# A decoder layer on one core: S5's outputs paused at the ninth batch, GLA heads cut in three, and the gate's adaLN loads spread anew

## The chip, the cores and the metric

The kernel runs on one core of a Trainium2 chip. The metric is the device time of one execution in microseconds (us). The core has a matrix engine (TensorE, PE in the profile; its weight loads are shown as PEld), a vector engine (VectorE, DVE), a scalar engine (ScalarE, ACT), a general engine (GpSimd, POOL) and a sync engine (SP) that here only issues DMAs. Each engine runs its own instructions strictly in the order in which they were written into its program, and waits at the first one whose inputs are not there. Sixteen DMA engines move data between the chip's memory and the on-chip buffer.

## The reference, cut to what matters

One layer of a hybrid decoder, in float32, with 256 tokens and a width of 4096:

```python
mod = silu(c) @ w_ada + b_ada;  shift, scale, gate = split(mod)      # adaLN, c is one row
h = x * (1 + scale) + shift
q, k, v, g_lr, z_gla, u_s5, z_s5 = split(h @ w_in)
# GLA, 4 heads: causal gated linear attention, RMS norm per head, times silu(z_gla)
# S5, 128 groups of 16 channels: s_t = A s_{t-1} + B u_t (complex, diagonal, 64 states)
y = gelu(Re(C s) + D u_s5);  y = y * sigmoid(y @ w_glu + b_glu);  o_s5 = y * silu(z_s5)
mixed = concat(o_gla, o_s5) @ w_out
out = layer_norm(ALPHA * x + gate * mixed)
```

Nearly all the weight traffic is w_ada (4096 x 12288), w_in (4096 x 10256), w_out (4096 x 4096) and w_glu (2048 x 2048). Only the product with w_ada has a single row on the left.

## The kernel before, in words

**Loads.** All large weights come in loads of 512 KB (128 partitions x 1024 numbers; two narrow chunks use less), issued on SP's queue into six buffers that all of them share in turn (raw, L81). A load of w_in, w_out or w_glu is split into two parts for a more exact product: ACT rounds it to hi (L114), DVE forms the rest as lo (L115). PE then multiplies three times, hi by hi, hi by lo and lo by hi. For w_in and w_out this is 12 matmuls of 512 columns a load (L211, L738), for w_glu 24 of 256 columns (L591). A load of w_ada goes to DVE alone: one instruction (L153; L151 for the first of a piece) multiplies it by its values of silu(c) and adds it to a running sum, rows, of which there is one buffer. 32 loads are a piece of 1024 columns; at its end PE sums over partitions with matmuls by a column of ones (L166 for shift and scale, L720 for gate). Pieces 0 to 7 are shift and scale, pieces 8 to 11 the gate, which is wanted only near the end.

**Stages.** First comes piece 0. Then w_in is multiplied in eight blocks b of the contraction, block by block as the pieces 1 to 7 arrive. It has 21 chunks of columns (KINDS, L45): four of u, S5's input; four of zs, S5's gate; then, for each of the four GLA heads, qk, v and zg (head 0's v is in two parts, va and vb). In the last block, b = 7, all chunks become final, the first eight (u and zs) with two loads each, the next six chunks with two, the last seven with four. A finished u chunk is turned by PE (L246) and rearranged by ACT with 32 small copies (L416); a finished zs chunk is turned and put through silu. Then follow: w_out's first half, on GLA's outputs (64 loads, eight chunks cc of eight); the GLU (32 loads); w_out's second half, on S5's outputs (64 loads); and the layer norm.

**S5** is a generator that is advanced beside the loads. s5_inputs makes the inputs of the state sums in 16 batches, and drives the first scan, of half of the states (scans[0]). s5_outputs then goes through the 16 batches again: s5_states (L506) multiplies the states by C on PE, s5_lags has PE turn a small matrix (L519) and ACT copy it out in 16 pieces (L522), and a last product (L552), an addition on DVE (L553) and 16 gelu pieces on ACT (L559) give y. A scan (s5_scan, L472) is a chain of 63 steps of four small DVE instructions (L479 to L482), each step on the one before. Batches 0 to 7 need scans[0]; batches 8 to 15 need scans[1], which s5_outputs itself drives, 12 steps an iteration, from its first iteration (L540, L547).

**Order.** Nothing of this order is fixed by the source alone. Each instruction has a priority, its place in the source, moved back by later(n); a planner, which runs ahead of time with its own idea of durations, puts together each engine's program from the instructions that it takes to be ready, by priority. The main function (hymba_layer) sets how fast the side work is brought in. Stages.step adds a rate to a sum and advances its generator by the whole steps in it. S5 gets RATES = (1.3, 0.85): s5_inputs 1.3 steps for each step of w_in's last 13 chunks (38 steps in all), s5_outputs 0.85 for each load of w_out's first half. The gate's w_ada loads (gate_steps, 128 loads and each piece's end) get GATE_RATES: 1.2 in the last block's u and zs chunks, 0 in the GLA chunks, 1.3 in w_out's first half from its fourth chunk on (nine steps a chunk), 0.9 for each GLU load, 0.7 in w_out's second half.

**GLA.** gla_head(h), L608, is one plain function, called after head h's zg chunk. It makes the decays (an exp, a log, an exp on ACT, L623 to L637; two scans on DVE, L628), turns q and k (L246), forms the attention matrix (L657, L661, L663), multiplies it by v (L670), norms and gates (L672 to L676), turns the result (L684) and splits it into hi and lo (L687, L688), which w_out's first half multiplies by.

Of the kernel before, what the change touches and what calls it, by code (L numbers as in the profile page):

```python
# [35 lines left out]

ADA_LEAD = 1

RATES = (1.3, 0.85)
GATE_RATES = (1.2, 0, 1.3, 0.9, 0.7)  # L40

PAIRED = (6, 7, 7, 7, 7, 8, 7)


KINDS = (  # L45
    [("u", i) for i in range(4)]
    + [("zs", i) for i in range(4)]
    + [("qk", 0), ("va", 0), ("vb", 0), ("zg", 0)]
    + [c for h in range(1, 4) for c in (("qk", h), ("v", h), ("zg", h))]
)  # L50
# [7 lines left out]
class Emit:  # L58
# [465 lines left out]
    def s5_outputs(self):  # L524


        nc = self.nc
        nb = NPAIR // NB
        self.y = []
        self.ct_next = None  # L530
        self.dd = [self.cp.tile([P, NB, 32], F32, name=f"dd{i}") for i in range(2)]
        for t in self.dd:
            nc.gpsimd.memset(t, 0.0)
        self.s5_prep(0)
        yield
        nxt = None
        for b in range(-1, nb):
            ys = nxt
            with self.later(-BG_LATE):
                drive(self.scans[1], 6)  # L540
            if b + 1 < nb:
                kt, nxt = self.s5_states(b + 1)
            if b + 2 < nb:
                self.s5_prep(b + 2)
            yield
            with self.later(-BG_LATE):
                drive(self.scans[1], 6)  # L547
            if b >= 0:
                o = self.zbank([P, NB, 64])
                for n in range(NB):  # L550
                    pr = b * NB + n
                    nc.tensor.matmul(o[:, n], lhsT=self.w0[b % 2][:, n], rhs=self.u4[pr // 16][:, pr % 16, :], start=True, stop=True)  # L552
                nc.vector.tensor_tensor(out=o, in0=o, in1=ys, op=ALU.add)  # L553
                if b % 4 == 0:
                    self.y.append(self.slot([P, 4, SEQ], name="y"))
                yv = self.y[-1][:, b % 4].rearrange("p (j c) -> p j c", j=4)
                for a in range(NB):
                    for j in range(4):
                        nc.scalar.activation(out=yv[32 * a : 32 * a + 32, j], in_=o[32 * j : 32 * j + 32, a], func=AF.Gelu_apprx_tanh)  # L559
                yield  # L560
            if b + 1 < nb:
                self.s5_lags(b + 1, kt)
                yield
# [42 lines left out]


    def gla_head(self, h):  # L608
        nc = self.nc
        v = nc.vector  # L610
        qk = self.acc["qk"][h]
# [49 lines left out]
        v.tensor_copy(out=att[:, 1], in_=ap[:, 1])  # L661
        for i in (0, 2):
            v.copy_predicated(att[:, i], self.causal.bitcast(U32), ap[:, i])  # L663
        zg = self.acc["zg"][h]
        ss = self.tmp([P, 2], "ss")
        ops = []
# [8 lines left out]
        for it in range(2):  # L675
            v.scalar_tensor_tensor(out=zg[:, it], in0=ops[it], scalar=rs[:, it : it + 1], in1=zg[:, it],  # L676
                                   op0=ALU.mult, op1=ALU.mult)
        o = zg
        hi = self.slot([P, 4, SEQ], F32R, "ohi")
        lo = self.slot([P, 4, SEQ], F32R, "olo")  # L680
# [131 lines left out]
def drive(g, n=1):  # L812

    for _ in range(n):
        if next(g, "end") == "end":
            return False
    return True
# [24 lines left out]
def chain(*gs):  # L842
    for g in gs:
        yield from g


def win_plan():

    nch = len(KINDS)
    paired = [[]]  # L850
    for b in range(1, 8):
        n = PAIRED[b - 1]
        paired.append(list(range(nch - n, nch) if b % 2 == 1 else range(n)))
    paired.append([])
    plan = []
    for b in range(8):
        pairs = [(n, [b - 1, b]) for n in paired[b]]
        alone = [(n, [b]) for n in range(nch) if n not in paired[b] + paired[b + 1]]
        plan.append(alone + pairs if b == 7 else pairs + alone)
    return plan  # L860


@with_exitstack
def hymba_layer(ctx: ExitStack, tc: tile.TileContext, io):
    em = Emit(tc, ctx, io)
    em.h = {}
    em.part = {}
    em.consts()
    em.alloc_acc()
    em.stats = em.cp.tile([P, 2, 8, 6], F32, name="stats")  # L870
    em.oh, em.ol = [None] * 8, [None] * 8

    drive(em.ada_steps(0), 99)
    with em.later(LATE):
        em.s5_params()
        em.ln_rows()
    em.u4 = []
    s5 = Stages((em.s5_inputs(), RATES[0]), (em.s5_outputs(), RATES[1]))
    nch = len(KINDS)
    ada = chain(*[em.ada_steps(u) for u in range(1, 8)])  # L880
    plan = win_plan()
    marks, at = [], 0
    for b, visits in enumerate(plan):
        marks.append(at)
        at += sum(len(us) for _, us in visits)
    marks[0], pos, done = 0, 0, 0
    gt = Stages((em.gate_steps(), 1))
    for b, visits in enumerate(plan):
        for n, us in visits:
            last = us[-1] == 7  # L890
            em.win_chunk(n, us, us[0] == 0, last)
            pos += len(us)
            want = round(33 * np.interp(pos + ADA_LEAD, marks, range(8)))
            drive(ada, want - done)
            done = max(done, want)
            kind, i = KINDS[n]
            steps = range(len(us) if kind in WIDTHS else 2 * len(us))
            if b == 7:
                for _ in steps:
                    gt.step(GATE_RATES[0] if n < S5_AT else GATE_RATES[1])  # L900
            if last and n >= S5_AT:
                with em.later(LATE):
                    for _ in steps:
                        s5.step()
                if kind == "zg":
                    em.gla_head(i)
    for cc in range(8):
        for i, _ in enumerate(em.wout(cc, 0)):
            if i < 8:
                with em.later(BG_LATE):  # L910
                    s5.step()

                gt.step(GATE_RATES[2] if cc > 2 else 0)
    s5.finish()
    em.glu_prepare()
    for cc in range(8):
        for _ in em.glu_chunk(cc):
            gt.step(GATE_RATES[3])
    left = []
    for cc in range(8):  # L920
        for i, _ in enumerate(em.wout(cc, 1)):
            gt.step(GATE_RATES[4])
            if i == 4 and left and len(em.gates) > left[0] // 2:
                em.residual(left.pop(0))()
        left.append(cc)
    gt.finish()
    for cc in left[:-1]:
        em.residual(cc)()
    em.layer_norm(em.residual(left[-1]))
# [69 lines left out]
```

## Time and profile before

| | us |
|---|---|
| median of three runs | 1723.9 (1722.66 to 1725.07) |
| the profiled execution, its own time | 1730.86 |
| its span, first to last instruction | 1729.1 |
| PE busy, of the span | 1546.0 (89%) |
| DVE busy | 1461.6 (85%) |
| ACT busy | 829.7 (48%) |
| mean share of the DMA engines | 78% (queues 1 and 0 together) |
| mean granted TensorE clock | 0.963 of full |

The profile is of one execution. A group of instructions is shown with its line, engine, operation, what it writes and reads, its count, its busy time and the mean of one, and then the idle time of its engine just before it with the engine that ended most of it. Matmuls are pipelined and overlap in the profile, so a PE that is shown busy need not be at its peak. A view by stretches gives, for each stretch, its length, the busy time and the count of instructions of PE, PEld, DVE, ACT and POOL, the clock granted to TensorE, the share of the DMA engines and the GB/s.

By the marks in the trace the last block's u and zs chunks end near 900, the GLA chunks near 1053, w_out's first half near 1415 (the GLU's first matmul is at 1415.29), the GLU near 1505, the gate's loads near 1625, and w_out's second half near 1700.

### The profile page before, as it was taken

The page shows a single profiled execution, that of the slowest core. Times are in us where ns is not written, and L with a number is a line of the kernel's source. Part 1 is how long each engine was busy: PE and PEld are TensorE (multiplying, and loading weights), DVE is VectorE, ACT ScalarE, POOL GpSimd, SP SyncE. Part 2 cuts the span into 40 slices and gives each one's busy share as a digit, 9 for nine tenths or more (in the row PEclk, how much of TensorE's full clock was granted, in tenths as well). Part 3 has the DMA queues.
Part 4 walks back from the last instruction along what each step waited for, and adds up shares of the span by engine and source line. Part 5 has one row for each costly group of instructions (what it writes and reads, how often), then busy time and mean ns, then how long its engine had stood idle before and what let it go on. Part 6 is the DMA issues. An engine that isn't in the chain of part 4 may idle for free.

```text
span 1729.1 us, 22283 instructions
## 1 busy us (share of the span) xinstructions
PE 1546.0 (89%) x7548; PEld 1285.3 (74%) x7548; DVE 1461.6 (85%) x2096; ACT 829.7 (48%) x1468; POOL 67.2 (4%) x134
## 2 busy tenths in 40 slices
PE   0689999999999999998989999889749889999995
PEld 0577878888888888877768888668637669977783
DVE  6899889898998999988867689979876779989975
ACT  0345434343343433433687767458538835433330
POOL 1000000000000000000001000000000000010100
PEclk9999999999999999999999999979969999999996
DMA  9999999999999999999876343317516899999962
GB/s 351 346 352 348 357 323 351 338 338 347 344 347 338 342 358 333 335 312 315 291 251 211 115 145 123 106 54 236 198 40 206 282 364 326 372 345 345 346 191 97
DMA packets 138067, 480.65 MB, mean 278 GB/s; under 512 B 17899, under 2 KB 18363, under 8 KB 137691
## 3 DMA queue, kind: packets, MB, share of 16 engines
q1 hardware_dynamic: 130240, 457.85, 74.0%
q0 software_dynamic: 7712, 21.37, 3.8%
q8 instruction: 59, 0.97, 0.2%
q14 instruction: 56, 0.46, 0.1%
HBM read 472.77 MB, written 6.39 MB: 277 GB/s over the span
## 4 chain that ended last, share of the span: by engine, by line
PE 65%; DVE 12%; ACT 9%; DMA 7%; issue 6%; SPq 0%; DVEq 0%; ACTq 0%
PE mm L211 42%; PE mm L738 13%; DVE rows L153 5%; DVE lo L115 3%; DMA raw<-in_ada 3%; ACT hi L114 2%; ACT u L416 2%; ACT w L522 2%; PE mm L591 2%; DMA raw<-in_w_out 2%; ACT y L559 2%; PE pz L506 2%; DMA raw<-in_w_glu 2%; PE pz L465 1%; PE px L166 1%
## 5 line engine op out<-in xcount | busy, mean ns | idle before, releaser
L114 ACT CAST hi<-raw 128x1024 fp32r<-128x1024 f32 (+2 forms) x496 | 506.6, 1025 | 626.2 <-DMA raw<-in_w_in 212.3
L115 DVE TENSOR_TENSOR lo<-raw,hi 128x1024 fp32r<-128x1024 f32 (+2 forms) x496 | 583.6, 1186 | 103.7 <-ACT hi L114 95.3
L211 PE MATMUL mm<-hi,hhi 128*128 128x512 f32 (+2 forms) x1344 | 512.8, 385 | 24.3 <-ACT hi L114 17.6
L211 PE MATMUL mm<-hi,hlo 128*128 128x512 f32 (+2 forms) x1344 | 511.5, 383 | 0.0
L153 DVE SCALAR_TENSOR_TENSOR rows<-raw,silu_c,rows 128x1024 f32<-128x1024 f32 x372 | 476.2, 1280 | 28.7 <-DMA raw<-in_ada 25.3
L211 PE MATMUL mm<-lo,hhi 128*128 128x512 f32 (+2 forms) x1344 | 353.1, 385 | 1.8 <-DVE lo L115 1.7
L211 PEld LDWEIGHTS mm<-hi,hhi 128*128 128x128 f32 x1344 | 254.8, 190 | 74.9 <-ACT hi L114 19.8
L211 PEld LDWEIGHTS mm<-hi,hlo 128*128 128x128 f32 x1344 | 255.0, 190 | 47.5
L211 PEld LDWEIGHTS mm<-lo,hhi 128*128 128x128 f32 x1344 | 247.2, 190 | 51.3 <-DVE lo L115 4.5
L738 PE MATMUL mm<-hi,ohi 128*128 128x512 f32 x512 | 209.3, 410 | 18.4 <-ACT hi L114 17.1
L738 PE MATMUL mm<-hi,olo 128*128 128x512 f32 x512 | 205.9, 403 | 0.0
L738 PE MATMUL mm<-lo,ohi 128*128 128x512 f32 x512 | 142.4, 400 | 6.4 <-DVE lo L115 6.4
L738 PEld LDWEIGHTS mm<-hi,ohi 128*128 128x128 f32 x512 | 99.5, 195 | 45.8 <-ACT hi L114 23.8
L738 PEld LDWEIGHTS mm<-lo,ohi 128*128 128x128 f32 x512 | 96.3, 191 | 32.4 <-DVE lo L115 10.9
L738 PEld LDWEIGHTS mm<-hi,olo 128*128 128x128 f32 x512 | 99.8, 195 | 20.5 <-issue 0.3
L506 PE MATMUL pz<-e,pad 128*128 128x97 f32 (+1 forms) x256 | 49.6, 361 | 32.1 <-issue 26.8
L506 PEld LDWEIGHTS pz<-e,pad 128*128 128x128 f32 x256 | 46.3, 239 | 35.8 <-issue 27.2
L591 PE MATMUL mm<-yhl,hi 128*128 128x256 f32 x512 | 68.3, 287 | 3.7 <-ACT hi L114 3.7
L591 PEld LDWEIGHTS mm<-yhl,hi 128*128 128x128 f32 x512 | 64.8, 195 | 5.5 <-ACT hi L114 4.6
L166 PE MATMUL px<-ones,rows 128*128 128x1 f32 x128 | 16.5, 258 | 54.8 <-DVE rows L153 54.8
L522 ACT COPY w<-px 32x128 f32<-32x128 f32 (+3 forms) x256 | 55.5, 217 | 15.9 <-PE px L519 11.6
L166 PEld LDWEIGHTS px<-ones,rows 128*128 128x128 f32 x128 | 17.2, 209 | 55.5 <-DVE rows L153 54.8
(238 smaller groups left out, 1197.9 us busy)
## 6 DMA issues: line engine op xcount, KB each, us to landing
raw<-in_ada SPq DMA_DIRECT2D x384, 512.0 KB, 5.5
raw<-in_w_in SPq DMA_DIRECT2D x304, 512.0 KB, 5.3
raw<-in_w_out SPq DMA_DIRECT2D x128, 512.0 KB, 4.8
raw<-in_w_glu SPq DMA_DIRECT2D x32, 512.0 KB, 5.7
raw<-in_w_vb SPq DMA_DIRECT2D x16, 272.0 KB, 3.8
x<-in_xT POOLq DMA_DIRECT2D x16, 256.0 KB, 4.9
raw<-in_w_va SPq DMA_DIRECT2D x16, 256.0 KB, 4.2
xo<-in_x_tok POOLq DMA_DIRECT2D x8, 512.0 KB, 7.0
```

The source lines that it names most:

```text
L114: nc.scalar.copy(out=hi, in_=src)
L115: nc.vector.tensor_tensor(out=lo, in0=src, in1=hi.bitcast(F32), op=ALU.subtract)
L153: nc.vector.scalar_tensor_tensor(out=rows, in0=t, scalar=c, in1=rows, op0=ALU.mult, op1=ALU.add)
L166: nc.tensor.matmul(ps[:, s, kt : kt + 1], lhsT=self.rows[:, 512 * s + kt * P : 512 * s + kt * P + P], rhs=self.ones[:, 0:1], start=True, s ...
L211: nc.tensor.matmul(ps[:, m, 0:w], lhsT=t[:, 2 * half + kt, m * P : m * P + P], rhs=r[:, kt], start=st, stop=en)
L416: nc.scalar.copy(out=self.u4[i][32 * j : 32 * j + 32, 8 * half + a : 8 * half + 8 : 4, :], in_=uv[32 * a : 32 * a + 32, :, j, :])
L465: nc.tensor.matmul(eps[:, ri, :, n], lhsT=w1s[n // 2][:, n % 2, ri], rhs=self.u4[pr // 16][:, pr % 16, :], start=True, stop=True)
L506: nc.tensor.matmul(yps[:, n, 0 : moved.shape[1]], lhsT=pad[:, n, ri].rearrange("p k g h -> p (k g h)"), rhs=moved[:, :, ri, (b * NB + n) % ...
L522: nc.scalar.copy(out=w0[32 * j : 32 * j + 32, n, 32 * j : P], in_=kps[32 * n : 32 * n + 32, 0 : P - 32 * j])
L559: nc.scalar.activation(out=yv[32 * a : 32 * a + 32, j], in_=o[32 * j : 32 * j + 32, a], func=AF.Gelu_apprx_tanh)
L591: nc.tensor.matmul(ps[:, m], lhsT=w[:, kt, m * P : m * P + P], rhs=t[:, kt, :], start=u == 0 and j == 0, stop=u == 3 and j == len(todo) - 1)
L738: nc.tensor.matmul(ps[:, it], lhsT=t[:, 2 * n2 + m, it * P : it * P + P], rhs=w[:, m], start=first and j in (0, 2), stop=last and j >= len ...
```

## The change

Four things, and no instruction's size or count of the arithmetic changes:

- **S5's outputs.** The rate rises from 0.85 to 0.92 steps a load, and at the head of the iteration that makes the states of batch 8, the ninth, the generator yields nine times and does nothing.
- **GLA heads.** gla_head becomes a generator with two yields. Its first part, up to the attention matrix, is now run after the head's qk chunk (head 0: after vb); its second part, the product with v, the norm and the gate, after the zg chunk, where the whole head stood; its third, the turn and the split, one chunk later, and for the last head after four loads of w_out's first chunk.
- **u and zs.** Their eight chunks come in turn: u0, zs0, u1, zs1 and so on. Their loads' order in memory follows.
- **The gate's loads.** The rates become 1.2, 0.4, 1, 0.9 and 0.6.

```diff
-RATES = (1.3, 0.85)
-GATE_RATES = (1.2, 0, 1.3, 0.9, 0.7)
+RATES, PAUSE = (1.3, 0.92), 9
+GATE_RATES = (1.2, 0.4, 1, 0.9, 0.6)
...
-    [("u", i) for i in range(4)]
-    + [("zs", i) for i in range(4)]
+    [c for i in range(4) for c in (("u", i), ("zs", i))]
...
         for b in range(-1, nb):
             ys = nxt
+            if b == 7:
+
+                for _ in range(PAUSE):
+                    yield
             with self.later(-BG_LATE):
                 drive(self.scans[1], 6)
...
             v.copy_predicated(att[:, i], self.causal.bitcast(U32), ap[:, i])
+        yield
         zg = self.acc["zg"][h]
...
                                    op0=ALU.mult, op1=ALU.mult)
+        yield
         o = zg
...
+    turn = []
...
+                if turn:
+                    drive(turn.pop(), 9)
+                if kind == "vb" or kind == "qk" and i:
+                    head = em.gla_head(i if kind == "qk" else 0)
+                    drive(head)
                 if kind == "zg":
-                    em.gla_head(i)
+                    drive(head)
+                    turn.append(head)
...
                 gt.step(GATE_RATES[2] if cc > 2 else 0)
+                if cc == 0 and i == 3:
+                    drive(turn.pop(), 9)
```

## The prediction, made before the changed kernel was run

> **What bounds the kernel now.** I read the page first, for the engines and their slices, then stretches of it by stage, then the instructions around the largest gap.
>
> ```profile
> PE 1546.0 (89%) x7548; PEld 1285.3 (74%) x7548; DVE 1461.6 (85%) x2096; ACT 829.7 (48%) x1468; POOL 67.2 (4%) x134
> PE   0689999999999999998989999889749889999995
> PEclk9999999999999999999999999979969999999996
> DMA  9999999999999999999876343317516899999962
> ```
>
> PE is the busiest engine, but slices 20 to 32 hold its gaps, and there DMA is nearly empty. The stretches, with length first, then PE, PEld, DVE, ACT, POOL, clock, DMA share and GB/s:
>
> ```profile
> 850.00:900.00 50.00, 42.92 (x200) 34.44 (x199) 35.56 (x30) 45.88 (x143) 1.63 (x3) 0.93 0.77 249
> 900.00:1053.00 153.00, 153.00 (x866) 129.14 (x865) 113.76 (x234) 108.55 (x163) 12.43 (x26) 1.00 0.50 161
> 1053.00:1141.00 88.00, 76.01 (x388) 61.27 (x386) 80.73 (x290) 46.22 (x73) 4.92 (x11) 0.94 0.34 107
> 1141.00:1243.00 102.00, 94.80 (x457) 81.73 (x457) 81.80 (x195) 79.33 (x273) 4.81 (x9) 0.92 0.57 187
> 1243.00:1273.00 30.00, 3.19 (x13) 2.36 (x14) 27.50 (x148) 0.00 (x0) 0.00 (x0) 0.59 0.06 18
> 1273.00:1415.00 142.00, 119.73 (x516) 94.24 (x516) 104.16 (x119) 95.59 (x314) 7.46 (x13) 0.89 0.70 242
> 1505.00:1625.00 120.00, 113.70 (x521) 91.58 (x520) 108.80 (x100) 44.81 (x45) 10.07 (x19) 1.00 0.96 350
> 1625.00:1700.00 75.00, 74.53 (x324) 59.85 (x322) 50.39 (x48) 25.32 (x25) 4.79 (x9) 1.00 0.57 185
> ```
>
> The w_out first half is the weak stage. The four rows from 1053 to 1415 add to 362 us with PE busy for 293.7 and DVE for 294.2: both are idle for 68 us, in turn. The largest gap:
>
> ```profile
> 1272.82 0.50 PE L506 MATMUL pz<-e,pad 128*128 128x96 f32 x1 [26.81 <-issue]
> 1272.49 0.22 DVE L482 TENSOR_TENSOR e<-sc,sc 128x64 f32<-128x64 f32 x1
> L482 DVE TENSOR_TENSOR e<-sc,sc 128x64 f32<-128x64 f32 x34 | 7.6, 225 | 1.2
> ```
>
> The last row groups DVE from 1246 to 1273. The profile names "issue", but PE's next instruction is batch 8's states, and it starts 0.1 us after the scan step that ended at 1272.71. DVE did 34 steps in that gap and nothing else, 0.79 us a step. So the gap is the second scan, late; ACT, SP and the loads stood still behind it.
>
> One load of w_out costs PE 12 matmuls. In the last stretch, which is nearly all w_out, 324 took 74.53 us: 0.230 each, 2.76 a load. A w_ada load, 512 KB at the 350 GB/s of 1505 to 1625, is 1.5 us of DMA and 1.28 of DVE; the groups of DVE from 1053 to 1415, and in the last row w_ada's from 1142 to 1243:
>
> ```profile
> L115 DVE TENSOR_TENSOR lo<-raw,hi 128x1024 fp32r<-128x1024 f32 x63 | 76.8, 1220 | 32.9 <-ACT hi L114 32.0 <-PE mm L738 0.6 <-issue 0.2
> L153 DVE SCALAR_TENSOR_TENSOR rows<-raw,silu_c,rows 128x1024 f32<-128x1024 f32 x51 | 65.2, 1277 | 2.9 <-DMA raw<-in_ada 2.5
> L153 DVE SCALAR_TENSOR_TENSOR rows<-raw,silu_c,rows 128x1024 f32<-128x1024 f32 x13 | 16.6, 1275 | 1.5 <-DMA raw<-in_ada 1.3
> ```
>
> **The change part by part.** The sum is made against the profiled execution's own 1730.86 us (span 1729.1); the median of the runs is 7 below it, and I carry the difference over unchanged.
>
> *The pause.* Nine empty steps at 0.92 a load are 9.8 loads; PE has 9.8 x 2.76 = 27.0 us to do where it now stands for 26.8. What is queued behind batch 8's states on PE is w_out's matmuls, and with them ACT's hi, DVE's lo and SP's loads; these come in front of it. The price is on DVE: 9.8 loads bring 9.8 x 1.22 of lo and, at the new rate of 1, 9.8 x 1.28 of rows, 24.5 us, beside 34 steps x 0.79 = 27. Behind all of it the states would come some 25 us later, yet with ten loads more done. Bounds: 0, if the planner still lets PE wait as long, to -26.8. I take **-26.8**, since DVE's stretch of 1505 to 1625 shows 91% busy beside a PE at 95%.
>
> *The clock after it.* A stall is paid twice:
>
> ```profile
> 1270.00:1280.00 10.00, 7.18 (x27) 5.38 (x27) 6.60 (x25) 1.80 (x8) 0.05 (x1) 0.50 0.00 1
> 1280.00:1290.00 10.00, 8.43 (x44) 6.87 (x43) 6.06 (x11) 7.99 (x37) 2.53 (x5) 0.87 0.21 66
> 1290.00:1300.00 10.00, 6.37 (x19) 4.84 (x20) 9.78 (x13) 9.33 (x40) 0.48 (x1) 0.66 0.61 181
> ```
>
> Busy time by the share of the clock that was missing: 7.18 x 0.50 + 8.43 x 0.13 + 6.37 x 0.34 = 6.9 us. Some of it belongs to later small gaps; **-5**, bounds 0 and -6.9. The Trainium skill, "TensorE: Matmul & The Clock Gate", Part 1: The HAM clock gate, says that an idle array falls to half clock and is released after about 3.4 us of steady work: one restart would cost an estimated 1.7 us and the whole sum would be 3.3 us smaller. The three rows show a clock below full for longer, and I keep the rows.
>
> *GLA in parts.* The last head's chain now lies wholly before w_out's first chunks can end:
>
> ```profile
> 1089.31 1.28 ACT L624 ACT_TABLE_LOAD   x1
> 1123.40 0.48 PE L684 MATMUL px<-ident,zg 128*128 128x128 f32 x1 [4.16 <-DVE zg L676]
> 1141.76 0.58 PE L506 MATMUL pz<-e,pad 128*128 128x97 f32 x2 [3.74 <-DVE e L482]
> wg<-in_w_gla_gate POOLq DMA_DIRECT2D x4, 16.0 KB, 2.4
> ```
>
> From 1053 to 1141 PE is idle for 88 - 76.0 = 12.0 us. Of this 3.7 is the wait of batch 0's states for the first scan; the rest, 8.3, lies in and around head 3. With its first part two chunks (eight loads, 22 us) earlier, most goes: **-8**, bounds 0 and -12. Each head's small load (2.4 us to landing) and its two fills on POOL's queue move with its first part, past loads of S5's parameters; the 22 us hide them, and without that cover the head pays the 2.4. The tables that ACT loads are as many as before.
>
> *The gate's loads.* By the rates, w_out's first half has 45 instead of 58.5, the GLA chunks 38 x 0.4 = 15.2 instead of none, and the tail 19.8 after the GLU instead of 21.5, over 33 loads instead of 31. In w_out's first half DVE loses 13.5 x 1.28 = 17.3 us; PE gains only where DVE is last: **-4**, bounds 0 and -17.3. In 900 to 1053 PE is full, DMA half empty and DVE 39 us idle, so the 15.2 x 1.28 = 19.5 us fit; but each new load takes one of the six buffers on SP's queue until DVE is done with it, ahead of w_in's. **+4**, bounds 0 and +19.5. In the tail (1505 to 1625: DMA 0.96, DVE 91%) a load's share falls by 0.1 x 1.5 us, over 33 loads 5: **-3**, bounds 0 and -5.
>
> *u and zs in turn.* From 850 to 900 ACT is the bound, 45.9 of 50:
>
> ```profile
> L416 ACT COPY u<-px 32x128 f32<-32x128 f32 x127 | 32.7, 257 | 1.6
> PE px L246 <- ACT u L416: 7.1, 5, 2.4
> ```
>
> The 128 copies come in a run and PE loses 50 - 42.9 = 7.1 us to them. Spread over eight chunks they need the same 33 us, over 16 loads x 2.76 = 44 us of PE: **-4**, bounds 0 and -7.1.
>
> *S5's end.* It has 50 steps, over 0.85 that is 58.8 loads; 59 over 0.92 is 64.1, all 64. What is late next is the last y, which the GLU needs:
>
> ```profile
> 1373.16 1.05 ACT L572 CAST yhl<-y 128x1024 fp32r<-128x1024 f32 x1
> 1415.29 0.38 PE L591 MATMUL mm<-yhl,hi 128*128 128x256 f32 x1 [2.04 <-ACT hi L114]
> L522 ACT COPY w<-px 32x128 f32<-32x128 f32 (+1 forms) x117 | 25.4, 217 | 8.7 <-PE px L519 6.1
> L559 ACT ACTIVATE y<-pz 32x64 f32<-32x64 f32 x112 | 24.1, 215 | 2.8 <-DVE pz L553 1.5
> ```
>
> Now the last cast of y begins 42 us before the GLU. Batches 8 to 15 took from 1273 to 1373. A last batch with nothing beside it is 16 x 0.217 + 16 x 0.215 = 6.9 us of ACT with a few us of PE and DVE between: **+8**, bounds 0 and +15.
>
> **Sum:** -26.8 - 5 - 8 - 4 + 4 - 3 - 4 + 8 = -38.8; 1730.9 - 38.8 = 1692 for an execution like the profiled one, 1723.9 - 38.8 = **1685** for the median. A second way, by S5 alone: batch 8 comes 24.5 us later for the paused loads, 8 earlier for head 3, and 4 earlier for the 13 rows that become 10, so some 12 us after 1273; its last y is 12 us after 1373, and a GLU right behind it starts 30 us before 1415. With u and zs, the tail and the GLA chunks, -4 - 3 + 4, that is 1691, within the range below.
>
> **The rivals.**
>
> *A. DVE takes the stall's place.* It is 92% busy both in 1053 to 1141 and in the gap. If the paused loads' 24.5 us push the scan back by as much, PE waits in many small pieces for DVE's lo instead of once for the scan, at the same cold clock, and of the first half's gains only DVE's saved rows count: -17.3 + 4 - 3 - 4 + 8 = -12, **1712**. Against it: the same rows show 68 us of idle DVE in the stage. By the Trainium skill, "Perfetto Trace Analysis", Identifying the Most-Contended Engine, occupancy is a fair measure for VectorE; it would name DVE in 1053 to 1273 and so speaks for this rival.
>
> *B. Slower: S5's chain outruns its cover.* The 15 rows in the GLA chunks push the first scan back by up to 19.5 us, the pause adds 27.0, and the last y comes 46.5 us later, near 1420. From 42 us on it is S5 and no longer w_out that sets the GLU's start, and all gains before it are lost; PE has no load left beside the last two batches, each 6.9 us of bare ACT: 4.5 + 13.8 = 18, against 7 saved in u, zs and the tail: +11, **1735**. For it: 64.1 steps for 64 loads. Against it: DVE's 39 idle us before 1053.
>
> *C. The pause does not do what it says.* The planner lets PE wait for the states behind the paused loads as long as before: the 26.8 and the 5 stay, and with S5's end at its bound the rest is -8 - 4 + 4 - 3 - 4 + 15 = 0: **1724**. For it: the wait of the profile was planned too, since DVE's program holds the 34 steps in one piece.
>
> *D. More.* DVE's 294.2 us in w_out's first half fall by 17.3; at the 91% of 1505 to 1625 the stage takes 305 us, 57 less; with -4 - 3 + 4 that is **1664**.
>
> **How the numbers follow.** The forecast has 0.53 (its own range 1668 to 1702), A 0.20, B 0.12, C 0.07, D 0.08. A change of 0.2%, 3.4 us, is about what a measurement of this kernel can tell from none. Faster is the forecast, A and D, 0.81; same is C, 0.07; slower is B, 0.12. The low end, 1652, is D with the bounds of the clock, 6.9, and of u, zs and the tail, 5; the high end, 1722, is A with S5's end at its bound, 7, and 3 more for the rows in the GLA chunks. The range leaves out B and most of C.
>
> **What would show it.** PE's wait before batch 8's states is under 5 us, with some ten more of w_out's loads done by then; the clock stays above 0.9 in the stage; in 1053 to 1141 no wait of PE on head 3 is above 2 us; 900 to 1053 has about 15 rows on DVE and PE still above 97%; the time from the last cast of y to the GLU's first matmul falls from 42 us to below 20. The forecast is wrong if that wait stays above 15 us, if PE in the GLA chunks falls below 90%, or if the GLU's start waits for y.

## The result and the profile after

The changed kernel takes 1703.25 us (median of four runs, 1702.25 to 1706.66) beside 1724.49 for the kernel before on the same chip: a ratio of 0.9866, 95% interval 0.9848 to 0.9883. It is 21 us faster by the medians and 23 by the ratio; 39 were forecast. Where parts are weighed against one another below, the ratio is taken, times 1725. The profiled execution took 1702.25, its span is 1700.4, so it stands 1 us below its median, whereas the one of before stood 7 above: between the two profiles lie 28.7 us, between the medians 21.

The page of the kernel after, engines and slices:

```profile
PE 1535.8 (90%) x7548; PEld 1282.5 (75%) x7548; DVE 1455.3 (86%) x2096; ACT 827.4 (49%) x1468; POOL 66.4 (4%) x134
PE   0689999999999999999899999869995879999995
PEclk9999999999999999999999999979997789999996
DMA  9999999999999999998997643314894079999962
```

Slices 26, 27 and 31 to 33 (42.5 us each) still hold holes in PE and in the clock, and DMA reads 1 and 0 at the bottom of them. The stretches of the kernel after, with the columns of before (length, PE, PEld, DVE, ACT, POOL, clock, DMA share, GB/s):

```profile
830.00:889.00 59.00, 55.35 (x274) 45.32 (x274) 52.33 (x49) 49.80 (x138) 3.79 (x7) 1.00 0.92 319
889.00:1053.00 164.00, 159.62 (x921) 134.67 (x921) 134.35 (x274) 116.05 (x188) 12.18 (x26) 1.00 0.58 188
1053.00:1141.00 88.00, 67.72 (x310) 51.60 (x310) 79.43 (x294) 38.46 (x72) 6.13 (x14) 0.85 0.31 97
1141.00:1287.00 146.00, 144.44 (x683) 121.51 (x681) 129.06 (x270) 101.50 (x286) 4.29 (x8) 0.98 0.76 264
1287.00:1306.00 19.00, 0.74 (x4) 0.38 (x3) 16.37 (x82) 2.09 (x2) 0.00 (x0) 0.64 0.30 99
1306.00:1330.00 24.00, 18.00 (x78) 16.91 (x78) 10.69 (x23) 16.61 (x73) 1.07 (x2) 0.50 0.02 6
1330.00:1384.00 54.00, 47.24 (x223) 39.21 (x222) 28.60 (x38) 46.45 (x179) 3.06 (x6) 0.84 0.40 136
1384.00:1488.00 104.00, 98.94 (x778) 96.12 (x778) 96.39 (x87) 56.12 (x96) 4.62 (x9) 0.97 0.91 329
```

The u and zs stretch of before, for the first row:

```profile
834.00:901.00 67.00, 56.57 (x262) 45.32 (x261) 51.56 (x48) 54.45 (x155) 2.58 (x5) 0.95 0.79 265
```

And the waits that matter, from the timeline of the kernel after (L505, L481, L575 and L594 are the L506, L482, L572 and L591 of before; L744, L114 and L152, further down, are its L738, L115 and L153):

```profile
1129.48 0.74 PE L505 MATMUL pz<-e,pad 128*128 128x97 f32 x2 [14.86 <-DVE e L481]
1305.62 1.60 PE L505 MATMUL pz<-e,pad 128*128 128x96 f32 x6 [18.26 <-DVE e L481]
1383.60 0.64 PE L594 MATMUL mm<-yhl,hi 128*128 128x256 f32 x4
1397.24 1.04 ACT L575 CAST yhl<-y 128x1024 fp32r<-128x1024 f32 x1
1398.34 0.58 PE L594 MATMUL mm<-yhl,hi 128*128 128x256 f32 x1 [3.39 <-ACT yhl L575]
```

The wait before batch 8 is there as before, 18.3 us instead of 26.8, behind the same instruction of the second scan; batch 8 starts 33 us later, at 1305.6 instead of 1272.8. What has changed is how much of w_out is done by then. w_out's matmuls (12 a load) before batch 8, in the kernel before and after:

```profile
1053.00:1272.80 219.80, 121.78 (x468) 0.88 0.41 132
```

```profile
1053.00:1305.60 252.60, 166.53 (x672) 0.91 0.57 194
```

39 loads have become 56, 17 more. By stages in us, from the marks in the two traces:

| stage | before | after | difference |
|---|---|---|---|
| up to the last addition to zs | 900.5 | 888.7 | -11.8 |
| GLA chunks, to w_out's first matmul | 153.2 | 164.7 | +11.5 |
| w_out's first matmul to batch 8 | 219.1 | 252.2 | +33.1 |
| batch 8 to the GLU's first matmul | 142.5 | 78.0 | -64.5 |
| GLU | 97.1 | 104.0 | +6.9 |
| from the GLU's last matmul to the end | 216.7 | 212.8 | -3.9 |

### The profile page after: what moved, and what is told of

Read it like the earlier page. It is cut to its first block, busy times and chain, and to the rows that moved or that the text cites. A ratio compares the mean times of both kernels' runs of the same rounds, so it can differ in the third digit from the quotient of the medians.

```text
span 1700.4 us, 22243 instructions
## 1 busy us (share of the span) xinstructions
PE 1535.8 (90%) x7548; PEld 1282.5 (75%) x7548; DVE 1455.3 (86%) x2096; ACT 827.4 (49%) x1468; POOL 66.4 (4%) x134
## 4 chain that ended last, share of the span: by engine, by line
PE 61%; DVE 16%; ACT 9%; DMA 8%; issue 5%; SPq 0%; DVEq 0%; ACTq 0%; POOLq 0%
PE mm L210 40%; PE mm L744 11%; DVE rows L152 5%; DMA raw<-in_ada 4%; DVE lo L114 4%; PE mm L594 4%; ACT hi L113 2%; ACT y L562 2%; ACT w L521 2%; DMA raw<-in_w_in 2%; DMA raw<-in_w_out 2%; PE pz L505 2%; PE px L165 1%; DVE sc L478 1%; DVE e L481 1%
## 5 line engine op out<-in xcount | busy, mean ns | idle before, releaser
L114 DVE TENSOR_TENSOR lo<-raw,hi 128x1024 fp32r<-128x1024 f32 (+2 forms) x496 | 582.8, 1184 | 72.5 <-ACT hi L113 66.8
L152 DVE SCALAR_TENSOR_TENSOR rows<-raw,silu_c,rows 128x1024 f32<-128x1024 f32 x372 | 475.7, 1279 | 38.6 <-DMA raw<-in_ada 35.5
L744 PE MATMUL mm<-hi,ohi 128*128 128x512 f32 x512 | 204.1, 400 | 4.9 <-ACT hi L113 4.9
L744 PE MATMUL mm<-hi,olo 128*128 128x512 f32 x512 | 202.5, 397 | 0.3 <-DVE olo L694 0.2
L744 PE MATMUL mm<-lo,ohi 128*128 128x512 f32 x512 | 141.3, 397 | 2.1 <-DVE lo L114 2.1
L744 PEld LDWEIGHTS mm<-hi,ohi 128*128 128x128 f32 x512 | 97.3, 191 | 28.3 <-ACT hi L113 7.4
L744 PEld LDWEIGHTS mm<-lo,ohi 128*128 128x128 f32 x512 | 96.2, 190 | 25.4 <-DVE lo L114 4.6
L744 PEld LDWEIGHTS mm<-hi,olo 128*128 128x128 f32 x512 | 97.4, 191 | 21.5 <-DVE olo L694 1.4
L505 PE MATMUL pz<-e,pad 128*128 128x97 f32 (+1 forms) x256 | 51.7, 375 | 33.1 <-DVE e L481 33.1
L505 PEld LDWEIGHTS pz<-e,pad 128*128 128x128 f32 x256 | 48.8, 266 | 35.2 <-DVE e L481 34.0
L594 PE MATMUL mm<-yhl,hi 128*128 128x256 f32 x512 | 70.2, 291 | 4.6 <-ACT yhl L575 3.4
L594 PEld LDWEIGHTS mm<-yhl,hi 128*128 128x128 f32 x512 | 66.5, 199 | 6.2 <-ACT yhl L575 3.6
```

What stands on the lines that cost most here:

```text
L114: nc.vector.tensor_tensor(out=lo, in0=src, in1=hi.bitcast(F32), op=ALU.subtract)
L152: nc.vector.scalar_tensor_tensor(out=rows, in0=t, scalar=c, in1=rows, op0=ALU.mult, op1=ALU.add)
L505: nc.tensor.matmul(yps[:, n, 0 : moved.shape[1]], lhsT=pad[:, n, ri].rearrange("p k g h -> p (k g h)"), rhs=moved[:, :, ri, (b * NB + n) % ...
L594: nc.tensor.matmul(ps[:, m], lhsT=w[:, kt, m * P : m * P + P], rhs=t[:, kt, :], start=u == 0 and j == 0, stop=u == 3 and j == len(todo) - 1)
L744: nc.tensor.matmul(ps[:, it], lhsT=t[:, 2 * n2 + m, it * P : it * P + P], rhs=w[:, m], start=first and j in (0, 2), stop=last and j >= len ...
```

## The experiments

**Each part alone.** The kernel before with one of the four parts.

The pause and 0.92 (e1):

```diff
-RATES = (1.3, 0.85)
+RATES, PAUSE = (1.3, 0.92), 9
...
+            if b == 7:
+                for _ in range(PAUSE):
+                    yield
```

> The kernel before with S5's new rate (0.92) and its pause of nine loads alone. If the pause is what lets PE multiply in front of batch 8's states (the pause theory, as predicted), the wait before batch 8 falls from 26.8 us to below 10 and the time falls by 15 to 25 us. If that wait was held open by the end of a gate piece - the one buffer rows is not free, four of the six load buffers fill with w_ada, and w_out's loads stop (the piece-end theory) - the pause alone leaves it near 25 us and the time moves by less than 8 us either way.

Measured: 1733.5 beside 1727.7, ratio 1.0041 (1.0020 to 1.0061). Alone, the pause makes the kernel slower, by 7 us. Batch 8 starts at 1333, 60 us later than before, with 56 loads in front, and still after a wait of 29.7 us. The pause and the rate of 0.92 go together in every run here; "the pause" below means both, and what each does by itself was not tried.

The GLA heads in three parts (e3), the edit as in the change:

> The kernel before with GLA's heads in three parts alone. Predicted: -8 us, head 3's first part two chunks earlier. From the trace after the change, where the heads' first matmuls come at 912, 976, 1030 and 1081 us against 924, 979, 1036 and 1085 before, the other view is that the heads follow one another as before and this part brings less than 4 us.

Measured: 1725.9 beside 1727.7, ratio 0.9991 (0.9972 to 1.0011): no change that can be told from none. Inside, batch 0 starts 9 us earlier (1132.7 instead of 1141.8), but batch 8 only 2.5.

The gate's rates (e4):

```diff
-GATE_RATES = (1.2, 0, 1.3, 0.9, 0.7)
+GATE_RATES = (1.2, 0.4, 1, 0.9, 0.6)
```

> The kernel before with the gate's new rates alone. Pause theory: -4 +4 -3, so about -3 us, and batch 8 still waits 20 us or more. Piece-end theory: the piece no longer ends while batch 8 waits for the scan; PE multiplies on, more than 45 loads of w_out's first half are done when batch 8's states start (39.6 in the kernel before), and the time falls by 15 us or more.

Measured: 1727.6 beside 1727.7, ratio 0.9995 (0.9974 to 1.0017): no change that can be told from none. Yet its trace has moved: batch 8 starts at 1308.3, behind a wait of 33.2 us, with 48 loads in front instead of 39. The piece-end theory has its loads here and not its time.

u and zs in turn (e5), the new KINDS:

> The kernel before with u and zs in turn alone. Predicted: -4 us, PE's idle time of 7.1 us beside ACT's 128 copies shrinks, and the last of u and zs ends some 4 us earlier than 900.5. The other view, from the parts run so far (each alone moved the time by -2 to +7 us though their sum is -23 together): the few us are taken back where the second scan sets the start of batch 8, and the time moves by less than 3 us.

Measured: 1715.0 beside 1725.4, ratio 0.9941 (0.9918 to 0.9964). A line that the forecast priced at 4 us brings 10. Its stage ends 9 us earlier, but the GLA chunks behind it then take 167 us instead of 153, with the gate's loads as before. The groups of S5's inputs on PE in the GLA chunks, first the kernel before (901 to 1053), then u and zs alone (891 to 1058):

```profile
L465 PE MATMUL pz<-u,w 128*128 128x64 f32 x168 | 21.1, 268 | 0.0
L452 PE MATMUL pz<-ident,pad 128*128 128x128 f32 x87 | 14.6, 273 | 0.0
```

```profile
L464 PE MATMUL pz<-u,w 128*128 128x64 f32 x196 | 26.6, 275 | 0.0
L451 PE MATMUL pz<-ident,pad 128*128 128x128 f32 x100 | 15.8, 279 | 0.0
```

41 more of S5's small matmuls stand there, 6.7 of the 14 us: work has moved over the stage's edge. w_out's first matmul comes 5 us later than before, and the stage behind it is 14 us shorter (347.6 from there to the GLU, instead of 361.6). A gain that is read at one mark can be lost or doubled at the next, and only the end counts.

**Two parts together, and one part undone.** The four alone add to 7.1 - 1.6 - 0.9 - 10.2 = -5.6 us; together they give -23. So some depend on one another. The pause together with the gate's rates (e9):

> The kernel before with the pause (and 0.92 steps a load) and the gate's new spread; GLA heads and the order of u and zs stay as before. Pause alone took 1733.5 with batch 8 at 1333, gate alone 1727.6 with batch 8 at 1308. Theory: the second scan is late because rows and splits of DVE stand between its steps; with 1.0 row a load in place of 1.3 it ends earlier, batch 8 starts near 1315 with some 57 loads in front, and the pause then pays: 1712 to 1718. Rival: the gate's spread doesn't matter for the scan, which comes whenever the loads in front are through; the other two parts make the difference: batch 8 above 1328 and 1725 to 1735.

Measured: 1717.7 beside 1727.9, ratio 0.9938 (0.9923 to 0.9953). The time is the first theory's: two edits that give +7 and -1 us alone give -11 together. Batch 8 is at 1321.6, 7 us later than that theory said, again with 56 loads in front.

The changed kernel with the gate's old rates (e10):

```diff
-GATE_RATES = (1.2, 0.4, 1, 0.9, 0.6)
+GATE_RATES = (1.2, 0, 1.3, 0.9, 0.7)
```

> The changed kernel with the gate's old spread (1.2, 0, 1.3, 0.9, 0.7). Theory (rows beside the scan): batch 8 moves from 1306 to 1320 or later, and the time from 1703 to 1710 to 1716. Rival: the gate's spread is neutral, and what the rows cost in the GLA chunks (13 us) they give back in the tail: batch 8 within 5 us of 1306, 1700 to 1706. By the prediction's own terms (-4, +4, -3) 1706.

Measured: 1723.2 beside 1727.9, ratio 0.9979 (0.9967 to 0.9991). Without the gate's spread all but 4 us of the gain are gone, more than either theory gave it.

The changed kernel without the pause, at 0.85 (e2):

```diff
-RATES, PAUSE = (1.3, 0.92), 9
+RATES, PAUSE = (1.3, 0.85), 0
```

> The changed kernel with S5's old rate (0.85) and no pause; GLA's parts, u and zs in turn and the gate's new rates stay. Pause theory: it loses 15 to 25 us against the changed kernel, so it takes about 1722 us. Piece-end theory: it keeps most of the gain, 1695 to 1710 us, since the gate's new rates put the piece's end elsewhere, and S5's last batches have more loads beside them.

Measured: 1714.7 beside 1727.7, ratio 0.9927 (0.9904 to 0.9951). The pause is worth 10.5 us here, less than the pause theory gave it and more than the other, and it costs 7 where the gate is as before.

The changed kernel with each head in one go (e12), gla_head without its yields, called behind zg:

> The changed kernel with each GLA head issued in one go behind its zg, as before. The prediction gave the parts 8 us: 1711. The traces say otherwise: head 3's first matmuls came 4 us earlier than before, all of it from u and zs, and the part alone took 0.9991 of before: 1701 to 1705, with the heads' first matmuls within 3 us of 913, 976, 1030 and 1081.

Measured: 1704.0 beside 1727.9, ratio 0.9859 (0.9844 to 0.9874), the same as with the parts. Head 3's first matmul is at 1086 instead of 1081, batch 8 at 1306.3 instead of 1305.6.

Why the pause and the gate need one another is read from two stretches of each kernel: from w_out's first matmul to batch 8, and from there to the GLU. Pause alone:

```profile
1053.00:1333.00 280.00, 227.14 (x1063) 184.01 (x1062) 248.78 (x682) 146.93 (x367) 11.73 (x24) 0.89 0.58 201
1333.00:1412.00 79.00, 62.21 (x300) 53.80 (x300) 35.30 (x60) 66.05 (x263) 3.13 (x6) 0.78 0.20 62
```

Pause and gate:

```profile
1057.00:1322.00 265.00, 222.61 (x1063) 182.97 (x1062) 235.56 (x675) 149.05 (x372) 12.21 (x25) 0.91 0.55 188
1322.00:1401.00 79.00, 65.85 (x302) 56.28 (x301) 40.33 (x63) 63.96 (x255) 4.13 (x8) 0.76 0.30 97
```

The changed kernel with the gate undone:

```profile
1046.00:1317.00 271.00, 215.46 (x1023) 174.10 (x1022) 242.36 (x654) 144.90 (x364) 12.36 (x24) 0.91 0.58 206
1317.00:1396.00 79.00, 62.33 (x302) 54.14 (x303) 36.16 (x62) 66.91 (x265) 3.13 (x6) 0.78 0.20 62
```

And without the pause:

```profile
1052.00:1299.00 247.00, 193.31 (x896) 156.94 (x894) 216.36 (x634) 132.61 (x350) 10.52 (x22) 0.88 0.53 182
1299.00:1401.00 102.00, 87.28 (x406) 73.92 (x407) 52.56 (x78) 80.71 (x301) 4.66 (x9) 0.84 0.36 119
```

And the gate's rates alone:

```profile
1050.00:1308.00 258.00, 202.18 (x965) 165.62 (x963) 227.70 (x663) 140.20 (x362) 12.20 (x25) 0.89 0.51 177
1308.00:1410.00 102.00, 87.23 (x404) 74.02 (x405) 52.36 (x78) 80.57 (x301) 4.57 (x9) 0.84 0.35 116
```

The first stretch has DVE busy for 88 or 89% of it in all five; in the kernel before it is 190.0 of 220, 86% (the prediction's rows from 1053 to 1273), in the changed one 224.9 of 253, 89%. In order of length the seven kernels are in order of DVE's work, from 190 to 249 us, but not of PE's. The second stretch does not go with DVE's work: it is 142 us long with 25 loads left, 102 with 16 and 78 or 79 with 8, and DVE is idle for about half of the short ones. So each load that the pause brings forward in the kernel before saves 63 / 17 = 3.7 us behind and costs DVE's lo and its share of the rows in front. The rows instructions on DVE before batch 8, in the kernel before, with the pause alone, and with pause and gate (length, DVE busy and count, clock, DMA share, GB/s):

```profile
1053.00:1273.00 220.00, 16.57 (x13) 0.88 0.41 132
```

```profile
1053.00:1333.00 280.00, 56.22 (x44) 0.89 0.58 201
```

```profile
1057.00:1322.00 265.00, 39.61 (x31) 0.91 0.55 188
```

With 17 loads more, lo takes 17 x 1.22 = 21 us more; the rows take 40 more with the old rates and 23 with the new. That is 61 and 44 us of DVE, and the stretch grew by 60 and 45. Against 63 saved behind, and 7 or 4 lost in the GLU to a later last y, the pause alone gains nothing, and with the new rates it gains some 14 in the profile. Most of the missing rows (12) are done in the GLA chunks. The gate's rates alone already put 9 loads and 18 rows more in front than before, which makes the first stretch 38 us longer and the second 40 shorter. The pause on top of them adds 8 loads and no row: the first stretch grows by 7 us, the second shrinks by 23 and the GLU grows by 5, a gain of 11.

**The second scan taken away.** If DVE is the bound before batch 8, the second scan's 44 us there (56 steps of 0.79) should come off the time; if the pause only covers the late scan, it should be worth nothing without it. The second scan is cut to 7 of 63 steps in the changed kernel (e6), and in the one without the pause (e7):

```diff
-        for c in range(1, 64):
+        for c in range(1, 8 if h else 64):
```

> The changed kernel with the second scan cut to 7 of its 63 steps, so 56 x 0.79 = 44 us of DVE work are left out. If the second scan's end is what starts batch 8 (the scan theory), the 18.3 us wait goes, batch 8 starts 30 us or more earlier, and the time falls by 10 to 25 us. If something else holds batch 8 or the GLU, the time falls by less than 5 us.

> The changed kernel without pause and with S5's old rate, and with the second scan cut to 7 steps as in the run beside it. If the pause pays only because it puts loads in front of a late scan, it is worth nothing here: this run is within 4 us of the one with the pause, or faster. If the pause is worth its 10 us by itself, by spreading S5 over the loads, this run is about 10 us slower than the one with the pause.

Measured: 1669.6 and 1680.4 beside 1725.4, ratios 0.9671 (0.9650 to 0.9692) and 0.9735 (0.9716 to 0.9753). The cut is worth 34 of its 44 us, more than was expected, and batch 8 waits for nothing. Yet the pause is still worth 11 us, so covering the scan is not what it pays by here. What it does pay by is not shown: the order is planned anew, and the two runs differ by only 2.3 loads in front of batch 8 (35.0 and 32.7). Its gain lies behind batch 8, where e6 takes 121.6 us to the GLU's first matmul and e7 135.8. The two stretches of e6:

```profile
1050.00:1234.00 184.00, 162.61 (x795) 133.86 (x795) 149.44 (x398) 120.90 (x343) 11.66 (x24) 0.92 0.45 148
1234.00:1356.00 122.00, 115.69 (x555) 95.86 (x553) 89.01 (x101) 86.06 (x267) 4.66 (x9) 0.99 0.76 266
```

DVE's share falls to 81%, PE's rises to 88%, and behind batch 8 PE is at 95% with a full clock.

**The second scan on GpSimd.** The same work, all of it, on the idle engine (e8):

```diff
-        v, e = self.nc.vector, self.e[h]
+        v, e = self.nc.gpsimd if h else self.nc.vector, self.e[h]
```

> The changed kernel with the second scan's four instructions a step issued on GpSimd, which is idle 96% of the time, instead of DVE; the arithmetic is the same. Scan theory: the chain no longer lies between DVE's lo and rows, DVE has 50 us less to do in w_out's first half; if a step takes under 1.7 us on GpSimd, batch 8 starts before 1270 instead of 1305.6, its wait is under 5 us, and the time falls by 10 to 25 us. If a step takes over 2.5 us there, the chain is later than now and the time rises.

Measured: 1702.3 beside 1725.4, ratio 0.9852 (0.9826 to 0.9878): as with the scan on DVE, so the gain of 10 to 25 us did not come. The stretch before batch 8, and from views of the scan's instructions on POOL (ns: lowest, median, highest) and of PE:

```profile
1056.00:1280.00 224.00, 168.62 (x798) 135.72 (x796) 158.43 (x367) 124.76 (x343) 142.52 (x270) 0.88 0.46 155
```

```profile
L480 POOL TENSOR_TENSOR sc<-sc,e x22: 307/318/1356, 1239.7 to 1280.9; 128x64 f32<-128x64 f32 x22
```

```profile
1280.36 0.96 PE L505 MATMUL pz<-e,pad 128*128 128x96 f32 x3 [28.22 <-POOL e L481]
```

DVE is down to 71%, but the scan now takes from 1131.8 to 1281.7 on POOL, and batch 8 waits 28 us for it with 40 loads done instead of 56. In the last 41 us an instruction of 0.32 us takes up to 1.36 beside DVE's work. The Trainium skill, "SBUF — State Buffer", Who interferes with whom, says that a DVE instruction with two inputs in the buffer contends with a GpSimd instruction that reads it, since its second input comes through the read interface that the two engines share. These rows agree: 1.36 is 0.32 and most of the length of one rows or lo (1.22 to 1.28), as if the instruction had waited for the rest of it.

Those 28 us were then offered ten loads, with PAUSE at 18 (e11):

> The changed kernel with the second scan on GpSimd and a pause of 18 steps in place of 9. With 9 its scan ended at 1282 behind a wait of 28 us with 40.5 loads done, and took 1702. Theory (what counts is how many loads stand in front of batch 8 by the time that the scan is there): ten more loads of 2.8 us fill the 28 us, batch 8 starts at 1282 to 1290 with about 50 loads, and the time falls to 1680 to 1690. Rival: the loads put in front bring their splits to DVE, GpSimd's steps beside them slow down, and the scan moves back as far as the loads fill: batch 8 above 1300, still behind a wait above 10 us, 1697 to 1710.

Measured: 1716.8 beside 1727.9, ratio 0.9938 (0.9917 to 0.9960), slower than with 9. The stretch before batch 8 and the one behind:

```profile
1058.00:1298.00 240.00, 195.60 (x910) 158.51 (x908) 181.61 (x382) 134.92 (x352) 158.18 (x267) 0.90 0.53 184
1298.00:1395.00 97.00, 81.60 (x378) 68.43 (x378) 58.22 (x76) 68.67 (x249) 6.25 (x15) 0.85 0.57 197
```

Fifty loads are now in front, and batch 8 has moved from 1280 to 1298: the scan goes back as the rival says, PE still waits 20.5 us for it, and the time is even above the rival's range. In front 16 us are lost and behind 12 saved; the GLU takes 107 us instead of 100, and the last y comes at 1412. That is 16 - 12 + 7 = 11 of the 15 us by which the longer pause is slower. No run that does all the work is clearly faster than the changed kernel.

## Why the prediction was right, and where it was not

The direction was right and the range held the time; the size was off by 18 us, and the mechanism of the largest term was not the one forecast. Eight of the 18 lie in the comparison itself: the prediction carried the 7 us between the profiled execution and the median over to the new kernel, whose profiled execution stands 1 us below its median. By profiles, 1692 was forecast and 1702 came. The other ten lie in the steps. Read by the ratios of the runs instead, all 18 lie in them: the pause, the gate and S5's end came 16 us short, GLA 8 short, and u and zs 6 over. That the last error went the other way is luck, and the range held the time because it reached past rival A's 1712, not because the largest term was right.

**The pause, -26.8.** This step failed. It set ten loads' 27 us of PE into the 26.8 us in which PE stood, and let DVE's 24.5 us for them lie beside the scan. But that wait was DVE's own work, 27.5 busy of 30; what needs DVE there makes the wait come later. The groups on DVE in the 41 us before PE runs dry, kernel after:

```profile
L114 DVE TENSOR_TENSOR lo<-raw,hi 128x1024 fp32r<-128x1024 f32 x15 | 18.3, 1217 | 0.0
L152 DVE SCALAR_TENSOR_TENSOR rows<-raw,silu_c,rows 128x1024 f32<-128x1024 f32 x12 | 15.3, 1276 | 0.3 <-DMA raw<-in_ada 0.3
L481 DVE TENSOR_TENSOR e<-sc,sc 128x64 f32<-128x64 f32 x16 | 3.5, 218 | 0.1
```

And in the 19 us of the wait:

```profile
L481 DVE TENSOR_TENSOR e<-sc,sc 128x64 f32<-128x64 f32 x20 | 4.5, 224 | 0.6
L114 DVE TENSOR_TENSOR lo<-raw,hi 128x1024 fp32r<-128x1024 f32 x2 | 2.4, 1222 | 1.4 <-ACT hi L113 1.4
```

In the first DVE has no idle time, and a scan step takes 41 / 16 = 2.6 us because a lo or a row stands between its instructions; the last 20 steps take 19 us, two lo among them, when PE has nothing left. In every run with the whole second scan PE waits for it, for 18 to 33 us, wherever batch 8 starts. Rival A had this mechanism (the paused loads push the scan back), but not its form: PE still waits in one piece, and the gain is made behind batch 8. The rule of the Trainium skill that stood beside it, "Perfetto Trace Analysis", Identifying the Most-Contended Engine, pointed at DVE by its occupancy; 86 to 89% in seven kernels agrees.

**The gate's loads, -4 + 4 - 3.** The +4 and the -3 fit: the rows in the GLA chunks cost 164.7 - 157.5 = 7 us (after against e10) or 3 (e9 against e1), with PE at 97% of 889 to 1053, and the tail is 4 shorter. The -4 in w_out's first half is mis-sized. 13 fewer rows there (44 to 31) are worth nearly all of their 17 us of DVE, 280 - 265 = 15; -17.3 was the bound. The bound had it, the sum did not.

**Pause, gate and S5's end together:** -26.8 - 5 - 4 + 4 - 3 + 8 = -26.8 by the steps, -11 by e9.

**S5's end, +8.** About right: the GLU takes 6.9 more, 3.4 of it the wait on the last yhl at 1398. The last y came 24 us after 1373 where the second way had 12, and the GLU began before it.

**The clock, -5.** Wrong. From 1306 to 1330 the clock is 0.50, and by the prediction's formula the stretch from 1306 to 1384 loses 18.0 x 0.50 + 47.24 x 0.16 = 16.6 us, more than the 13.2 (119.73 x 0.11) from 1273 to 1415 before. With loads gone from beside S5, PE has 8 loads in 78 us to fill the gaps between batches. Over the whole span the mean clock is as before, 0.964 beside 0.963.

**GLA in parts, -8.** Wrong: 0 by e3 and by e12. Head 3 starts 4 us earlier, not 22: in both kernels the heads' first matmuls follow each other at 49 to 63 us (924, 979, 1036, 1085 before, 913, 976, 1030, 1081 after), and just before head 3's PE waits 2.40 us for head 2's last olo. PE's other idle time from 1053 to 1141 fell from 8.3 to 5.4 us (88 - 67.7 - 14.9), but the first scan's wait has grown from 3.7 to 14.9. Without the parts (e12) that wait is 3.7 again and batch 0 starts at 1135.1, 6 us later, while batch 8 starts 0.7 later: what the parts gain at batch 0 is gone by batch 8, which waits for the second scan. What holds the heads at this distance was not tried.

**u and zs, -4.** Under-sized: -10 by e5. In the changed kernel PE's waits on ACT's copies fell from 7.1 to 0.3 us (the stretch of 67 us became 59), as the step said. Its bound of -7.1 was that idle time alone and left out the clock, which went from 0.95 to 1.00 over 56.57 us of PE: an estimated 2.8 us more.

By what would show it: the wait is 18 us, not under 5, and the prediction named above 15 as its failure; 17 loads more instead of ten; the clock in the stage 0.87 instead of above 0.9; about 12 rows and 97% in the GLA chunks, as said. Rival B's first half did not come (the first scan ends at 1129, earlier than before), rival C's mechanism did not come, since the pause brings loads in front (56 for 39 in e1) and pays in e2 and e9, though in e1 PE waits as long as before; rival D is refuted by DVE at 89% before batch 8 and half idle behind it.

## What to carry to other kernels

Before filling an engine's wait, look at what the engine that ends it is doing: if that one is busy throughout, only work that it has no part in can be put there without moving the wait. Loads that cost two engines belong where both have room, so price a move at both ends, by what the stretch left behind is worth with fewer of them and by what the bound engine of the new stretch must do. Edits that share a bound engine are to be tried together as well as alone: here +7 and -1 made -11.

## What the runs showed of the hardware

After the wait for the second scan the clock stayed at half for 28 us, though PE was at work for most of them. The kernel after, PE's own stretches behind the wait (length, PE busy, clock, DMA share, GB/s):

```profile
1306.00:1309.60 3.60, 3.60 (x19) 0.50 0.00 0
1309.60:1313.00 3.40, 3.40 (x18) 0.50 0.01 2
...
1326.50:1330.00 3.50, 3.50 (x12) 0.50 0.00 0
1330.00:1340.00 10.00, 10.00 (x45) 0.83 0.19 55
```

PE's timeline at 1330 and at 1382, w_out's matmuls of 512 columns:

```profile
1330.07 0.63 PE L744 MATMUL mm<-hi,ohi 128*128 128x512 f32 x1
1330.50 0.63 PE L744 MATMUL mm<-hi,olo 128*128 128x512 f32 x1
...
1382.69 0.39 PE L744 MATMUL mm<-hi,ohi 128*128 128x512 f32 x1
1382.92 0.39 PE L744 MATMUL mm<-hi,olo 128*128 128x512 f32 x1
```

For 7 us from 1306 the profile shows PE busy without a gap, and the clock is not released; at 1330 such a matmul still starts 0.43 us after the last, at 1382 0.23. In the 24 us to 1330, all at half clock, PE was 75% busy, mostly with matmuls of 64 to 128 columns; the clock was full again at 1333.5. The rule that the prediction cited, the Trainium skill's "TensorE: Matmul & The Clock Gate", Part 1: The HAM clock gate (about 3.4 us of steady work), does not describe this.

Other runs differ. Without the pause (e2) the same instructions follow the wait, and after 8.3 us of PE without a gap the clock was full for 3.3 us and then half again. In e8, where w_out's matmuls of 512 columns stand 3.4 us behind the wait, it was full 5.8 us after the wait and stayed so. What PE must do to count as busy was not tried.
